# A two-layer RWKV-7 / attention hybrid on one core: the recurrence's L and R in one tile, 128-partition stream transposes, the product with v turned around, and a new order

## The chip, the cores and the metric

The kernel runs on one core of one Trainium2 chip. The metric is device time in microseconds of that core, the median of several executions. The core has TensorE (PE in the profile, with its weight loads as PEld), VectorE (DVE), ScalarE (ACT), GpSimd (POOL), and SyncE (SP), whose queue issues the weight transfers. Each engine runs its own instructions in program order, and waits on semaphores of the others.

## The reference, cut to what matters

Two layers of: a SwiGLU block, a mixer with three branches, a second SwiGLU block, on 256 tokens of width 1024. The branches are an RWKV-7 recurrence run forwards and backwards (8 heads of 64), global attention and window attention (8 query heads and 2 key/value heads each).

```
for l in range(2):
    x = x + 0.5 * swiglu(rmsnorm(x, ffn1_norm[l]), ffn1_w_up[l], ffn1_w_down[l])
    p = rmsnorm(x, mix_norm[l]) @ w_in[l]
    p_rwkv, p_ga, p_wa, p_gate = split(p)
    # recurrence, per head, in both directions of time:
    #   sa    = state @ a_t
    #   state = state * w_t + sa (x) b_t + v_t (x) k_t ;  y_t = state @ r_t
    y_a = rwkv_mixer(p_rwkv, ...)
    y_b = softmax(q k^T) v            # global, q and k normed and rotated
    y_c = window softmax with a sink  # 128 tokens to either side
    g = sigmoid(p_gate)
    x = x + (g0 * (y_a @ w_o_rwkv) + g1 * (y_b @ w_o_ga) + g2 * (y_c @ w_o_wa)) @ w_out
    x = x + 0.5 * swiglu(rmsnorm(x, ffn2_norm[l]), ffn2_w_up[l], ffn2_w_down[l])
return rmsnorm(x, final_norm)
```

## The kernel before, in words

**Weights.** Every weight is read once, in units of 128 x 1024 (`Net.unit`, lines 68 to 93). SyncE loads a unit into `w_raw`; ACT or DVE rounds it to `w_hi` (lines 61 and 63), and DVE or POOL forms the rest `w_lo` (line 92). Each big product is three matmuls (`mm3`): high by high, high by low, low by high. There are three `w_raw`, four `w_hi` and four `w_lo` buffers, so an engine that makes a `w_hi` can wait until PE has used up an older one.

**Mixer.** `Mixer.run` (line 976) is eight families of generators, and the string `ORDER` says which takes its next step: Q, projections of the two attentions; R, projections of the recurrence (tile `rk`, token shift in `shifted`, line 604); A, scores and softmax; V, the product with v (`pv`, line 509); K and P, preparation; 0 to 3, the four units of the recurrence (two pairs of heads, each forwards and backwards); O, its end; F, gates (`gt`) and output projections (`wo`), which are work for PE that can stand anywhere. The table `ENG` names the engine of each copy and, for each weight unit, who makes its two parts: v (ACT, DVE), p (ACT, POOL), w (DVE, POOL), x (DVE, DVE). Within the limits of the string, the framework's scheduler places the instructions of each engine.

**Product with v** (lines 509 to 543). Each pair of heads has its probabilities transposed on PE (`ptp`) and copied to the tile `PT`. Then, for each head, each half of the queries and each half of the keys, `PT` is the stationary operand, 128 x 128, and v is streamed with 64 columns: eight products per pair. The result `yv` has queries on the partitions; DVE multiplies it by the reciprocal of the softmax sum (line 538), PE transposes it back (`yTp`), and ACT and DVE split it into high and low parts.

**One unit of the recurrence** (`wkv`, line 719). PE forms the chunk products `Lp`; DVE masks the two halves of each bank into two tiles, `LA` and `LR` (lines 743 and 744, 128 x 256 each). After the backward unit of a pair, one triangular system is solved for both directions ("solve" from here on): four stream transposes of 32 partitions each bring the diagonal blocks of `LA` together in the tile `sol` (line 767), 28 small dependent DVE instructions (lines 775 and 776) solve it, further transposes bring it back (lines 780 and 785), and PE goes on with the products `gp` (line 791), `tp`, `gp`, `tp`, `lv`, `tx`, `rm`, `st` and `y`. `gp` and all behind it need the solve. There is one solve for each pair, so two in a mixer and four in the kernel. `LA` is one buffer for both directions of a pair; `LR` has two.

Of the kernel before, what the change touches and what calls it, by code (L numbers as in the profile page):

```python
# [288 lines left out]
class Mixer:  # L289
# [79 lines left out]
    def att_begin(self):  # L369
# [15 lines left out]
        at3 = self.t([128, 2048], "at3", tag="LA")  # L385
# [4 lines left out]
        self.t1 = at3[:, 1024:1664]  # L390
# [61 lines left out]
    def att_tools(self, kind):  # L452
# [10 lines left out]
        def turn():  # L463
# [45 lines left out]
        def pv(pr):  # L509
# [9 lines left out]
            if pr % 2 == 0:  # L519
                state["y"] = n.acc([128, 2, 4, 64], "yv")  # L520
            y = state["y"]
            for e in range(2):
                for t in range(2):
                    for kt in range(2):
                        first = pr % 2 + e + t + kt == 0
                        i = n.mm(y[:, t, 2 * (pr % 2) + e, :], self.PT[e][:, kt, 128 * t:128 * t + 128], qk[kt][:, v], start=first, stop=(kt == 1), skip_group_check=True)
                        if first:
                            state["first"] = i
                        else:
                            n.tc.add_manual_dep(i.ins, state["first"].ins.name, mybir.DependencyInfo(mybir.DependencyClass.NoSync, mybir.DependencyReason.DATA), reason="start of the bank")  # L530
# [7 lines left out]
            V.tensor_tensor(yt.rearrange("p t (h c) -> p t h c", c=64), y, den[:, :, hs].unsqueeze(3).to_broadcast([128, 2, 4, 64]), ALU.mult)  # L538
            p = n.bank([128, 2, 256], "yTp")
# [3 lines left out]
            n.split(p, yT[0][:, 2 * kv:2 * kv + 2, :], yT[1][:, 2 * kv:2 * kv + 2, :])  # L543
# [25 lines left out]
    def rwkv_begin(self):  # L569
# [4 lines left out]
        pad = [scr[:, 260 * i:260 * i + 258] for i in range(2)]  # L574
        for p in pad:
            nc.gpsimd.memset(p[:, 0:1], 0.0)
            nc.gpsimd.memset(p[:, 257:258], 0.0)
        self.pads, self.npad = pad, 0

    def rwkv_proj(self):  # L580
        nc, n, w = self.nc, self.n, self.a["w_in"][self.l]
        for g in (3, 1, 0, 2):
            for j0 in (0, 2):
# [16 lines left out]
                for j in range(nch):  # L600
                    self.shifted(g, j0 + j, acc[j])
                yield

    def shifted(self, g, j, acc):
        nc, n = self.nc, self.n
        ch = 4 * g + j
        dst = self.LG[:, j, :] if g == 3 else self.RKV[:, g, j, :]
        i = self.npad = self.npad + 1
        p = self.pads[i % 2]
        nc.scalar.activation(p[:, 1:257], acc, AF.Copy, scale=self.c2[:, ch:ch + 1])  # L610
        nc.vector.scalar_tensor_tensor(dst, acc, self.c1[:, ch:ch + 1], p[:, 0:256], ALU.mult, ALU.add)  # L611
        nc.vector.tensor_tensor(dst, dst, p[:, 2:258], ALU.add)
# [106 lines left out]
    def wkv(self, u):  # L719
# [28 lines left out]
        for i in range(2):  # L748
# [7 lines left out]
            for h in range(2):  # L756
                n.copy("av"[h], dst[E[h], 1], b[1][E[1 - h]])
# [301 lines left out]
```

## Time and profile before

| | us |
|---|---|
| median of 3 runs (1503.72 to 1505.63) | 1504.91 |
| time of the profiled execution | 1505.69 |
| span of the profiled execution, first to last instruction | 1503.8 |

The profiled execution's own time is 1.9 us more than its span, and 0.8 us above the median. Its mean granted TensorE clock was 0.98.

| stretch of the span, us | what runs |
|---|---|
| 0 to 202 | layer 0, first SwiGLU |
| 202 to 545 | layer 0, mixer: to 300 projections, to 360 attention and gates, then the recurrence with the gates |
| 545 to 569 | layer 0, product with w_out |
| 569 to 965 | layer 0, second SwiGLU, and layer 1, first SwiGLU |
| 965 to 1308 | layer 1, mixer and w_out |
| 1308 to 1504 | layer 1, second SwiGLU |

How to read the views. The groups of instructions give line, engine, operation, tile written <- tiles read, shapes, count | busy us, mean ns of one | idle time of the engine before them, and what ended it. The waits give who waited for whom: total us, times, longest. The windows give, for a stretch, busy time and count of each engine, the granted TensorE clock, the DMA share and GB/s. The timeline gives start us, length us, and in brackets the engine's idle time before the row. A product of two float32 operands is one row in the order of instructions and two records in the profile (the order has 128 rows of `yv`, the profile 256). Records of PE overlap, so the rate of a run of them is read from its start to the start of the next row, not from the length of one record.

### The profile page before, as it was taken

Reading aid. Unit: us, or ns where it says so; the run is one execution under the profiler, and the core shown is the slowest. Engines: PE = TensorE matmul, PEld = TensorE weight load, DVE = VectorE, ACT = ScalarE, POOL = GpSimd, SP = SyncE. Lnnn points to the kernel's source line nnn. Section 1 sums busy time; section 2 is a strip of 40 time slices with the busy share of each in tenths; the row PEclk is TensorE's granted clock in tenths of the full one; section 3 lists DMA queues with packets and bytes.
Section 4 is the critical chain, followed back from the end, with each engine's and each line's share of the span. In section 5 each row is a group of like instructions: output and inputs, shape, how many; then the busy total and the mean of one; then the engine's idle time right before and its main releaser. Section 6 shows DMA issues by size and latency. Waiting matters only on the chain.

```text
span 1503.8 us, 25092 instructions
## 1 busy us (share of the span) xinstructions
PE 1425.9 (95%) x10170; PEld 1167.8 (78%) x10170; DVE 925.7 (62%) x1384; ACT 701.9 (47%) x1109; POOL 224.5 (15%) x203
## 2 busy tenths in 40 slices
PE   8999999999797999999999999999997979999997
PEld 6888878877575778888888888788785758788886
DVE  5455468765859666555465554778657685755543
ACT  6444335764333246444354443466642332554443
POOL 0000033223214110000000000432242132100001
PEclk9999999999899899999999999999998989999999
DMA  7666656323313146666666666553242121576653
GB/s 220 195 198 189 189 149 187 109 85 106 106 51 98 53 133 182 185 181 190 186 182 184 182 185 193 152 170 105 78 125 87 44 86 58 153 213 182 194 182 112
DMA packets 113432, 220.19 MB, mean 146 GB/s; under 512 B 7362, under 2 KB 32164, under 8 KB 113316
## 3 DMA queue, kind: packets, MB, share of 16 engines
q1 hardware_dynamic: 111328, 215.08, 47.7%
q10 hardware_dynamic: 1508, 2.58, 0.6%
q8 instruction: 80, 1.31, 0.4%
q0 software_dynamic: 480, 0.93, 0.3%
q14 instruction: 36, 0.29, 0.1%
HBM read 217.51 MB, written 1.05 MB: 145 GB/s over the span
## 4 chain that ended last, share of the span: by engine, by line
PE 69%; DVE 14%; issue 5%; ACT 5%; DMA 4%; POOL 3%; SPq 0%; POOLq 0%; ACTq 0%; DVEq 0%
PE up L51 26%; PE dn L51 18%; PE gt L51 5%; DMA w_raw<-in_ffn_w_up 3%; DVE w_lo L92 3%; PE rk L51 3%; PE tp L54 2%; PE wo L51 2%; PE yv L51 2%; ACT w_hi L61 1%; DVE sol L775 1%; PE tx L51 1%; DVE sol L767 1%; DVE sol L776 1%; PE pj L51 1%
## 5 line engine op out<-in xcount | busy, mean ns | idle before, releaser
L92 DVE TENSOR_TENSOR w_lo<-w_raw,w_hi 128x1024 fp32r<-128x1024 f32 (+1 forms) x348 | 427.0, 1229 | 343.3 <-ACT w_hi L61 342.4
L61 ACT ACTIVATE w_hi<-w_raw 128x1024 fp32r<-128x1024 f32 (+1 forms) x376 | 394.6, 1051 | 469.1 <-PE up L51 175.0
L51 PE MATMUL up<-w_hi,hT 128*128 128x512 f32 x1408 | 443.5, 394 | 0.0
L51 PEld LDWEIGHTS up<-w_hi,hT 128*128 128x128 f32 x1408 | 265.3, 189 | 53.9
L51 PE MATMUL up<-w_lo,hT 128*128 128x512 f32 x704 | 274.5, 391 | 0.0
L51 PE MATMUL dn<-w_hi,aT 128*128 128x512 f32 x704 | 218.2, 390 | 0.0
L92 POOL TENSOR_TENSOR w_lo<-w_raw,w_hi 128x1024 fp32r<-128x1024 f32 (+1 forms) x62 | 147.5, 2383 | 228.1 <-ACT w_hi L61 146.1
L51 PEld LDWEIGHTS up<-w_lo,hT 128*128 128x128 f32 x704 | 132.7, 188 | 28.2 <-DVE w_lo L92 1.1
L51 PEld LDWEIGHTS dn<-w_hi,aT 128*128 128x128 f32 x704 | 131.7, 188 | 26.8
L51 PE MATMUL dn<-w_lo,aT 128*128 128x512 f32 x352 | 138.0, 392 | 0.0
L51 PE MATMUL gt<-w_hi,hT 128*128 128x512 f32 x384 | 135.8, 418 | 2.3 <-DVE w_hi L63 2.3
L51 PE MATMUL rk<-hT,w_hi 128*128 128x256 f32 x480 | 88.2, 285 | 2.5 <-DVE RKV L611 2.5
L51 PEld LDWEIGHTS gt<-w_hi,hT 128*128 128x128 f32 x384 | 73.8, 195 | 20.6 <-issue 3.0
L51 PE MATMUL gt<-w_lo,hT 128*128 128x512 f32 x192 | 80.5, 419 | 2.5 <-DVE w_lo L92 2.5
L142 POOL TENSOR_SCALAR stat<-stat 128x1 f32<-128x1 f32 x14 | 3.5, 254 | 511.1 <-ACT gh L138 495.0
L51 PEld LDWEIGHTS rk<-hT,w_hi 128*128 128x128 f32 x480 | 75.3, 191 | 4.4 <-DVE RKV L611 2.9
L51 PEld LDWEIGHTS dn<-w_lo,aT 128*128 128x128 f32 x352 | 66.1, 188 | 14.8 <-DVE w_lo L92 1.4
L51 PE MATMUL rk<-hT,w_lo 128*128 128x256 f32 x240 | 67.9, 284 | 1.4 <-POOL w_lo L92 1.4
L51 PE MATMUL wo<-w_hi,yT 128*128 128x512 f32 x192 | 65.5, 407 | 0.0
L51 PE MATMUL pj<-w_hi,hT 128*128 128x512 f32 x192 | 62.0, 397 | 2.1 <-DVE LG L611 2.1
L51 PEld LDWEIGHTS rk<-hT,w_lo 128*128 128x128 f32 x240 | 45.8, 191 | 1.8 <-POOL w_lo L92 1.8
L51 PEld LDWEIGHTS gt<-w_lo,hT 128*128 128x128 f32 x192 | 37.5, 195 | 11.6 <-DVE w_lo L92 3.2
(238 smaller groups left out, 1833.8 us busy)
## 6 DMA issues: line engine op xcount, KB each, us to landing
w_raw<-in_ffn_w_up SPq DMA_DIRECT2D x160, 512.0 KB
w_raw<-in_w_in SPq DMA_DIRECT2D x102, 512.0 KB
w_raw<-in_ffn_w_down SPq DMA_DIRECT2D x88, 512.0 KB
w_raw<-in_ffn_w_up SPq DMA_DIRECT2D x32, 256.0 KB
w_raw<-in_w_out SPq DMA_DIRECT2D x16, 512.0 KB
w_raw<-in_w_o_ga SPq DMA_DIRECT2D x8, 512.0 KB
w_raw<-in_w_o_wa SPq DMA_DIRECT2D x8, 512.0 KB
w_raw<-in_w_o_rwkv SPq DMA_DIRECT2D x8, 512.0 KB
```

The source lines that it names most:

```text
L51: return self.nc.tensor.matmul(*a, **k)
L54: return self.nc.tensor.transpose(*a, **k)
L61: self.nc.scalar.activation(out, in_, AF.Copy, scale=1.0 if scale is None else scale)
L92: self.engine(on[1]).tensor_tensor(o, r, h.bitcast(F32), ALU.subtract)
L142: nc.gpsimd.tensor_scalar(self.ss[:, c:c + 1], self.ss[:, c:c + 1], 1.0 / D, EPS, ALU.mult, ALU.add)
L767: V.transpose(sol[p0:p0 + 32], src[p0:p0 + 32, :, 32 * b:32 * b + 32].rearrange("p g (u t) -> p t u g", u=2))
L775: V.tensor_tensor(tv, Dm[:, s + 1:16, s:s + 1].to_broadcast([128, m, s]), Dm[:, s:s + 1, 0:s].to_broadcast([128, m, s]), ALU.mult)
L776: V.tensor_tensor(Dm[:, s + 1:16, 0:s], Dm[:, s + 1:16, 0:s], tv, ALU.add)
```

## The change

**One tile for L and R.** `LL` (128 x 2 x 8 x 192) holds `LR` in columns 0 to 127 and `LA` in 128 to 191, with two buffers. One DVE instruction of 128 x 512 masks a whole bank. The scratch tiles of the attention move into the same two buffers.

**128-partition transposes.** Before a solve, `blocks` copies the diagonal blocks of `LA` of both directions (32 partitions x 256, eight copies per solve, on ACT or DVE by the table entry K) into the second half of `scr`; then one stream transpose of 128 x 512 stands in for the four of 32 partitions.

**Product with v.** v is now the stationary operand (128 x 64) and `PT` is streamed with 256 columns, four products per pair; the two heads go to the two halves of the output partitions, in turn. The result `yp` has queries along the free dimension. The reciprocals are therefore spread, transposed on PE (`rdp`, as many transposes as `yTp` had) and copied (table entry J, two copies of 128 x 512 per key/value head), and one DVE product follows.

**Smaller edits.** The last addition of the token shift is done for two channel blocks at once. Copies that had a fixed engine take it from the table (entries K, C, U, Y, H, J).

**Order and table.** `ORDER` and `ENG` are new throughout.

```diff
-ORDER = 'QQQQQRRQQQRRQAQQRRRAAKAQRRPARRAKRKPVAVAARFRARFPVVAAAA...'
+ORDER = 'QQQQQQRRQQRQKRRRQQARARAQARAKARRRKPVVAAARFARARVVPPAAAAA...'
-        LR = self.t([128, 2, 8, 128], "LRt", tag="LR", bufs=2)
+        LL = self.t([128, 2, 8, 192], "LL", bufs=2)
+        LR, LA = LL[:, :, :, 0:128], LL[:, :, :, 128:192]
+        self.LAs[d] = LA
+        if d == 1:
+            scr = self.scr = self.t([128, 1024], "sol", tag="bk", bufs=2)
+            blk = scr[:, 512:1024].rearrange("p (n g t) -> p n g t", n=2, g=8)
+        def blocks(i):
+            for e in range(2):
+                for h in range(2):
+                    p = slice(64 * e + 32 * h, 64 * e + 32 * h + 32)
+                    n.copy(self.take("K"), blk[p, i], self.LAs[i][p, e, :, 32 * h:32 * h + 32])
+        if d == 1:
+            blocks(0)
...
-                V.tensor_tensor(LA[:, e, gs, :], b[e][:, :, 64:128], ...)
-                V.tensor_tensor(LR[:, e, gs, 0:64], b[e][:, :, 0:64], ...)
+                V.tensor_tensor(two(LL[:, e, gs, :])[:, :, 0:3:2, :], two(b[e]), ...)
+            if d == 1 and q == 1:
+                blocks(1)
...
-            for e in range(2):
-                src = LAp[:, e].rearrange("p n g t -> p (n g) t")
-                for b in range(2):
-                    p0 = 64 * e + 32 * b
-                    V.transpose(sol[p0:p0 + 32], src[p0:p0 + 32, :, 32 * b:32 * b + 32].rearrange("p g (u t) -> p t u g", u=2))
+            V.transpose(sol, blk.rearrange("p n g (u t) -> p t u (n g)", u=2))
...
-                state["y"] = n.acc([128, 2, 4, 64], "yv")
+                state["y"], state["first"] = n.acc([128, 2, 256], "yp"), [None, None]
...
-            for e in range(2):
-                for t in range(2):
-                    for kt in range(2):
-                        i = n.mm(y[:, t, 2 * (pr % 2) + e, :], self.PT[e][:, kt, 128 * t:128 * t + 128], qk[kt][:, v], ...)
+            for kt in range(2):
+                for e in range(2):
+                    i = n.mm(y[E[e], pr % 2, :], qk[kt][:, v], self.PT[e][:, kt, :], ...)
...
-            V.tensor_tensor(yt..., y, den[:, :, hs]..., ALU.mult)
-            p = n.bank([128, 2, 256], "yTp")
+            n.copy(self.take("J"), yt..., den[:, :, hs]...)
+            p = n.bank([128, 2, 256], "rdp")
...
-            n.split(p, yT[0][:, 2 * kv:2 * kv + 2, :], yT[1][:, 2 * kv:2 * kv + 2, :])
+            n.copy(self.take("J"), yt, p)
+            V.tensor_tensor(yt, y, yt, ALU.mult)
+            n.split(yt, yT[0][:, 2 * kv:2 * kv + 2, :], yT[1][:, 2 * kv:2 * kv + 2, :])
...
-        nc.vector.tensor_tensor(dst, dst, p[:, 2:258], ALU.add)
+        nc.vector.tensor_tensor(dst, dst, self.pads[:, :m, 2:258], ALU.add)
```

What the engines then run is read from the order of their instructions, in three places of layer 0.

VectorE, the first solve. `LAt` and `LRt` are the two tiles of before, `sol` is the scratch in which the system is solved, `T` are PE's transposes of the unit's operands. Before:

```order
L743 TENSOR_TENSOR LAt<-Lp_3229,consts 128x256
L744 TENSOR_TENSOR LRt<-Lp_3229,consts 128x4x64
L767 STREAM_TRANSPOSE sol<-LAt 32x512 x2
L63 COPY LRt<-T_3252 64x8x64
L767 STREAM_TRANSPOSE sol<-LAt 32x512 x2
L63 CAST w_hi<-w_raw 128x1024
L770 SCALAR_TENSOR_TENSOR sol<-sol,consts 128x256
L715 TENSOR_TENSOR BK<-kkh,tha 128x8x64
```

VectorE at the same place now:

```order
L752 TENSOR_TENSOR LL<-Lp_3169,consts 128x4x2x64
L752 TENSOR_TENSOR LL<-Lp_3170,consts 128x4x2x64
L63 COPY sol<-LL 32x256 x2
L772 STREAM_TRANSPOSE sol<-sol 128x512
L63 COPY LL<-T_3195 64x8x64
L775 SCALAR_TENSOR_TENSOR sol<-sol,consts 128x256
L63 CAST w_hi<-w_raw 128x1024
L780 TENSOR_TENSOR sol<-sol 128x14
```

Two block copies and one transpose stand where four transposes stood; the other six block copies of this solve are on ScalarE.

ScalarE, the second solve, before (`gth` are the gates' tanh):

```order
L61 ACTIVATE w_hi<-w_raw 128x1024
L61 ACTIVATE LRt<-T_4245 128x8x64
L61 ACTIVATE LRt<-T_4246 64x8x64
L61 ACTIVATE w_hi<-w_raw 128x1024 x3
L951 ACTIVATE gth<-gt_4224 128x512
```

ScalarE at the same place now:

```order
L61 ACTIVATE w_hi<-w_raw 128x1024
L61 ACTIVATE sol<-LL 32x256 x2
L61 ACTIVATE LL<-T_4224 128x8x64
L61 ACTIVATE sol<-LL 32x256 x2
L61 ACTIVATE LL<-T_4225 64x8x64
```

The four block copies of the backward direction stand behind a `w_hi` and around a copy of `T`.

TensorE, the end of the second solve, before:

```order
L51 MATMUL gt_4700<-w_hi,hT_65 128x512
L51 MATMUL gt_4700<-w_lo,hT_65 128x512
L51 MATMUL gt_4700<-w_hi,hT_66 128x512
L51 MATMUL gp<-Tn,LAt 32x32 x64
L51 MATMUL tp_4464<-sol,Tn 32x32 x32
L51 MATMUL tp_4503<-sol,Tn 32x32 x32
```

TensorE at the same place now:

```order
L51 MATMUL gt_4349<-w_hi,hT_66 128x512
L51 MATMUL gp<-Tn,LL 32x32 x64
L51 MATMUL gt_4350<-w_hi,hT_65 128x512
L51 MATMUL gt_4350<-w_lo,hT_65 128x512
L51 MATMUL gt_4350<-w_hi,hT_66 128x512
L51 MATMUL tp_4441<-sol,Tn 32x32 x32
L51 MATMUL tp_4480<-sol,Tn 32x32 x32
```

Three products of a gate have moved between `gp` and `tp`. By count of rows, from the last `Lp` to the first `gp` PE now has 66 big products in the first solve of a mixer (67 before) and 45 in the second (57 before), and 16 more transposes `T` in the first. From the decay preparation of the last unit (`lw`, `la`) to the second solve's `gp`, it has 101 (96 before).

Over the whole kernel DVE makes 52 `w_hi` (34 before) and POOL 50 `w_lo` (62 before).

More of the change, by code (lines that the diff above doesn't have):

```diff
@@ L469, in turn @@
                 nc.scalar.activation(kT[kind][E[e], e, :], p[E[e], 0, :], AF.Copy)
-                V.tensor_copy(kT[kind][E[1 - e], e, :], p[E[e], 0, :])
+                n.copy(self.take("H"), kT[kind][E[1 - e], e, :], p[E[e], 0, :])
             for i in range(2):
@@ L519, in pv @@
             if pr % 2 == 0:
-                state["y"] = n.acc([128, 2, 4, 64], "yv")
+                state["y"], state["first"] = n.acc([128, 2, 256], "yp"), [None, None]
             y = state["y"]
-            for e in range(2):
-                for t in range(2):
-                    for kt in range(2):
[L525 to L530, printed above, removed]
+            for kt in range(2):
+                for e in range(2):
+                    first = state["first"][e] is None
+                    i = n.mm(y[E[e], pr % 2, :], qk[kt][:, v], self.PT[e][:, kt, :], start=first, stop=(kt == 1), skip_group_check=True)
+                    if first:
+                        state["first"][e] = i
+                    else:
+                        n.tc.add_manual_dep(i.ins, state["first"][e].ins.name, mybir.DependencyInfo(mybir.DependencyClass.NoSync, mybir.DependencyReason.DATA), reason="start of the bank")
             if pr % 2 == 0:
@@ L537, in pv @@
             yt = self.yt[kv]
-            V.tensor_tensor(yt.rearrange("p t (h c) -> p t h c", c=64), y, den[:, :, hs].unsqueeze(3).to_broadcast([128, 2, 4, 64]), ALU.mult)
-            p = n.bank([128, 2, 256], "yTp")
+            n.copy(self.take("J"), yt.rearrange("p t (h c) -> p t h c", c=64), den[:, :, hs].unsqueeze(3).to_broadcast([128, 2, 4, 64]))
+            p = n.bank([128, 2, 256], "rdp")
             for r in range(2):
@@ L573, in rwkv_begin @@
         scr = self.t([128, 520], "projpad", tag="gth", bufs=2)
[L574 to L578, printed above, removed]
+        self.pads = scr.rearrange("p (i c) -> p i c", i=2)
+        nc.gpsimd.memset(self.pads[:, :, 0:258:257], 0.0)
     def rwkv_proj(self):
@@ L810, in wkv @@
         for e in range(2):
-            nc.scalar.activation(Gt[64 * e + 32:64 * e + 64], gp[64 * e + 32:64 * e + 64], AF.Copy)
+            n.copy(self.take("U"), Gt[64 * e + 32:64 * e + 64], gp[64 * e + 32:64 * e + 64])
         yield
@@ L817, in wkv @@
         for e in range(2):
-            V.tensor_copy(TT[64 * e:64 * e + 32, :, 32:64], tp[64 * e:64 * e + 32])
+            n.copy(self.take("U"), TT[64 * e:64 * e + 32, :, 32:64], tp[64 * e:64 * e + 32])
         b = n.bank([128, 8, 64], "lv")
@@ L824, in wkv @@
         for e in range(2):
-            (V.tensor_copy if e else nc.scalar.copy)(Z[E[e], e, :, 64:128], b[E[e]])
+            n.copy(self.take("Y"), Z[E[e], e, :, 64:128], b[E[e]])
         yield
@@ L833, in wkv @@
                 dst = Z[E[e], e, 4 * q:4 * q + 4, :].rearrange("p c (h t) -> p c h t", h=2)[:, :, ::-1, :]
-                (V.tensor_copy if e else nc.scalar.copy)(dst, b[E[e]].rearrange("p c (h t) -> p c h t", h=2))
+                n.copy(self.take("Y"), dst, b[E[e]].rearrange("p c (h t) -> p c h t", h=2))
             yield
```

45 lines of the change are left out of this document (19 added, 26 removed).

## The prediction

> **What bounds the kernel now.** I read the page's busy times, then the windows by stage, then who PE waits for inside the mixer, then the timelines there.
>
> ```profile
> span 1503.8 us, 25092 instructions
> PE 1425.9 (95%) x10170; PEld 1167.8 (78%) x10170; DVE 925.7 (62%) x1384; ACT 701.9 (47%) x1109; POOL 224.5 (15%) x203
> ```
>
> The windows by stage (us of the stage; busy us and count of PE, PEld, DVE, ACT, POOL; clock; DMA):
>
> ```profile
> 201.60:300.00 98.40, 91.75 (x594) 79.34 (x593) 77.88 (x124) 56.00 (x107) 33.80 (x40) 1.00 0.53 155
> 300.00:360.00 60.00, 58.45 (x369) 47.34 (x371) 35.79 (x75) 38.55 (x96) 21.22 (x12) 1.00 0.29 84
> 360.00:460.00 100.00, 88.53 (x1261) 69.93 (x1256) 68.24 (x134) 33.05 (x56) 20.52 (x11) 0.93 0.30 88
> 460.00:545.00 85.00, 73.69 (x1060) 60.35 (x1061) 63.22 (x120) 28.21 (x45) 26.22 (x13) 0.92 0.26 79
> 569.00:960.00 391.00, 387.98 (x1753) 315.68 (x1752) 215.73 (x244) 185.93 (x239) 14.49 (x31) 1.00 0.62 184
> ```
>
> The SwiGLU blocks (last row, 99% PE) are bound by PE, and the change doesn't touch them. In the mixer PE is 97% busy from 300 to 360, so work taken from PE there shows; from 360 to 545 it loses 22.8 us of 185. Of that, the largest wait is this one; its group for the whole kernel is below it:
>
> ```profile
> PE gp L51 <- DVE Tn L785: 12.5, 2, 7.3
> L51 PE MATMUL gp<-Tn,LAt 32*32 32x32 f32 x768 | 14.1, 224 | 29.3 <-DVE Tn L785 27.2 <-issue 2.1
> ```
>
> The four solves cost 27.2 us of PE's time: it has run out of gate products and waits for VectorE's chain. After each wait the clock is low, which makes the price a little higher:
>
> ```profile
> 400.00:410.00 10.00, 4.30 (x195) 3.93 (x196) 7.77 (x14) 0.15 (x1) 0.00 (x0) 0.52 0.34 108
> 490.00:500.00 10.00, 8.75 (x276) 7.54 (x278) 6.30 (x13) 3.31 (x8) 0.56 (x1) 0.53 0.17 56
> ```
>
> **The product with v.** PE's timeline, each row paired with the start of the next, gives rates:
>
> ```profile
> 349.17 2.00 PE L51 MATMUL yv<-att,at 128*128 128x64 f32 x16 [0.18 <-ACT at L61]
> 350.97 0.48 PE L51 MATMUL gt<-w_hi,hT 128*128 128x512 f32 x1
> ...
> 289.11 1.27 PE L51 MATMUL sc<-qkT 64*128 64x256 f32 x8
> 290.31 0.44 PE L54 MATMUL ptp<-head,at 128*128 128x128 f32 x2
> ...
> 426.16 0.92 PE L51 MATMUL st<-Zt,LRt 128*64 128x64 f32 x24
> 426.91 1.10 PE L51 MATMUL y<-LRt,Zt 128*64 128x64 f32 x32
> ...
> 496.41 1.91 PE L51 MATMUL bonp<-pz,consts 128*128 128x256 f32 x4
> 498.11 1.62 PE L51 MATMUL gatep<-LG,lora 128*128 128x256 f32 x4
> ```
>
> A `yv` record takes 1.80 / 16 = 0.112 us, so the 256 of them 28.8 us. The new form has 128 records of 256 columns on a 128 x 64 operand, which the trace doesn't show. Lower bound: `st` has that operand, two output halves in turn, and 0.75 / 24 = 0.031 us for 64 columns; four times the columns make 0.125, in all 16 us. Upper bound: `bonp`, 256 columns on a full operand, 1.70 / 4 = 0.425 us at clock 0.53, so 0.225 at full clock and 28.8 us: no gain. I take `sc`, 256 columns on half operands in turn, 1.20 / 8 = 0.150 us: 19.2 us, a gain of 9.6.
>
> Against it stand changes of the operand's shape, which the old form didn't need:
>
> ```profile
> 376.75 0.39 PE L51 MATMUL gt<-w_lo,hT 128*128 128x512 f32 x1
> 376.97 0.39 PE L51 MATMUL gt<-w_hi,hT 128*128 128x512 f32 x1
> 377.29 1.10 PE L51 MATMUL Lp<-ARV,BK 64*64 64x128 f32 x32
> ```
>
> Two `gt` start 0.22 us apart, `gt` and the differently shaped `Lp` 0.32: 0.10 us per change. The new order has ten groups of `yp` in a layer, so 40 changes in and out in all, 4 us. The term is -9.6 + 4 = **-5.6 us**; bounds -12.8 without a price for the changes, +4 with the upper bound.
>
> The Trainium skill's page "TensorEngine Tiling (Array Packing)", section Tiling Modes, speaks against this edit: changing the tiling mode drains TensorE. It gives no figure; the rows show 0.10 us, not an emptied pipeline (the `gt` record is 0.39 us long). Were every change to cost the rest of such a record, 0.39 - 0.22 = 0.17 us, 40 would be 7 us and the term -2.8.
>
> The spreading of the reciprocals adds 16 copies of 128 x 512 and takes nothing off PE (as many transposes). They need only the softmax sums, and lie on engines that are 60 and 64% busy in the window from 300 to 360: nothing; without that cover 16 x 0.69 = 11 us.
>
> **The solves.** VectorE's groups (and ScalarE's of 32 x 256, the nearest row for a block copy):
>
> ```profile
> L767 DVE STREAM_TRANSPOSE sol<-LAt 32x512 f32<-32x512 f32 x16 | 17.4, 1086 | 0.2
> L780 DVE STREAM_TRANSPOSE sol<-sol 128x512 f32<-128x512 f32 x4 | 4.2, 1038 | 0.1
> L803 ACT ACTIVATE TT<-sol 32x256 f32<-32x256 f32 x32 | 13.3, 414 | 47.1 <-DVE sol L799 46.8
> L743 DVE TENSOR_TENSOR LAt<-Lp,consts 128x256 f32<-128x256 f32 x32 | 13.3, 415 | 8.7 <-PE Lp L51 8.6
> L538 DVE TENSOR_TENSOR att<-yv,at 128x512 f32<-128x512 f32 x8 | 5.5, 691 | 15.2 <-PE yv L51 15.2
> L92 DVE TENSOR_TENSOR w_lo<-w_raw,w_hi 128x1024 fp32r<-128x1024 f32 x344 | 422.4, 1229 | 343.3 <-ACT w_hi L61 342.4
> ```
>
> Four transposes at 1.086 become one at 1.038: -3.3 us of chain. Two masks of 0.415 become one of 0.691 (`L538`, as many columns out of the same memory, is its nearest row): -0.14 per bank.
>
> *First solve of a mixer.* ScalarE has six block copies in a row, 6 x 0.414 = 2.5 us. They stand behind a copy of `T`, which I put at 0.7 (as `L538`), and that waits for PE's 16 transposes (0.5 at `st`'s 0.031): 3.7 us from the last `Lp`. VectorE's last two masks and two copies (0.4 each, as `L803`) take 2.2, so the transpose waits about 1.5 us: chain -3.3 + 1.5 = -1.8. PE's cover grows by 16 `T` (0.5) less one product (0.22): -0.3. Products now stand between `gp` and `tp`, where PE had nothing to do (the 2.1 of issue in the group above is one such gap): three fill 0.7. In all **-2.8 us** per layer of the 7.3. Bounds: -7.3 (the wait is gone) and +1 (the copies come later than the transposes were long).
>
> *Second solve.* VectorE is 63.22 of 85 us busy from 460 on, 9.2 of 10 just ahead of `gp`:
>
> ```profile
> 480.00:490.00 10.00, 4.89 (x34) 3.73 (x32) 9.21 (x30) 1.36 (x2) 4.02 (x2) 0.95 0.35 105
> ```
>
> From the last unit's preparation to `gp` its list gets shorter: -4.3 + 1.0 (transposes), -0.6 (eight masks of 0.415 to four of 0.691), -0.7 (one `w_hi`, row below) + 1.2 (one `w_lo`), + 0.4 (a block copy), and -2.2 for four instructions of 256 to 512 columns that now stand ahead of it (0.55 each, between `L743` and `L538`): -5.2 us. ScalarE's four copies come ahead of the transpose, + 1.4 on the chain. Between the last `Lp` and `gp` PE has twelve products less to cover the wait (2.6 us), but five more in the whole piece, work that it is spared elsewhere: I count these as equal. That leaves -3.8, say **-4 us** per layer; bounds -11 (PE's whole loss from 460 to 545) and +2 (the cover is lost, and little is gained).
>
> What can stretch the chain is seen here:
>
> ```profile
> 477.44 0.20 DVE L775 TENSOR_TENSOR sol<-sol 128x36 f32<-128x36 f32 x1
> 477.67 2.36 DVE L776 TENSOR_TENSOR sol<-sol 128x36 f32<-128x36 f32 x1
> ...
> 477.59 2.38 POOL L92 TENSOR_TENSOR w_lo<-w_raw,w_hi 128x1024 fp32r<-128x1024 f32 x1 [3.31 <-ACT w_hi L61]
> ```
>
> A `w_lo` on POOL holds a VectorE instruction that takes 0.2 us otherwise for 2.36. The new table has 12 fewer of them, but still some in the solves: no change taken.
>
> Both solves, two layers: 2 x (-2.8 - 4) = **-13.6 us**. With shorter waits the slow-clock stretches shorten: about 0.5 us at each, **-2**.
>
> **The rest.** VectorE makes 18 more `w_hi`, 13.4 us over two mixers where it is 60 to 79% busy by the windows:
>
> ```profile
> L63 DVE CAST w_hi<-w_raw 128x1024 fp32r<-128x1024 f32 x34 | 25.1, 743 | 13.1 <-PE gt L51 7.1 <-DMA w_raw<-in_w_in 2.8 <-issue 2.7
> ```
>
> Against them goes one of two additions in the token shift (15 per layer become eight, longer ones). I take nothing; up to 4 us per layer if the stage from 202 to 300 (VectorE 79%) becomes bound by it. POOL now has a `w_lo` between the sums of the last norm, 2.4 us, in a gap of 4.91:
>
> ```profile
> 202.22 0.30 POOL L142 TENSOR_SCALAR stat<-stat 128x1 f32<-128x1 f32 x1 [4.91 <-ACT gh L138]
> ```
>
> Nothing; without that gap 2.4 us per layer. Two `LL` buffers in place of one `LA` and two `LR`: no row has VectorE waiting for `LA`, so nothing. The fixed copies that now have an entry in the table: an engine change each, nothing.
>
> **The sum.** -5.6 - 13.6 - 2 = -21.2 us on the profiled execution's 1505.7: 1484.5. That execution was 0.8 above the median, so **1483.7 us**.
>
> **Rivals.**
> 1. *Deeper.* The waits for the solves nearly vanish (of 27.2, 25 go) and `yp` runs at its lower bound (-12.8): 1505 - 38 = 1467. For it: 101 products of cover before the second solve. Against it: only 45 of them behind the last `Lp`. 0.17.
> 2. *`yp` doesn't overlap.* The upper bound (+4), solves and clock as forecast (-15.6): 1493. For it: `bonp`. Against it: `st`. 0.13.
> 3. *The waits only move.* The order gives PE its cover elsewhere, and `gp` waits as long as before, while in the attention ACT's softmax, not PE, ends last: 1504. For it: twelve products fewer before the second `gp`. 0.06.
> 4. *Slower: the block copies wait behind ScalarE's `w_hi`.* Place: the ScalarE rows at the second solve, and the six copies at the first. ScalarE's waits in the mixer:
>
> ```profile
> ACT w_hi L61 <- PE gt L51: 13.0, 5, 5.3
> ACT LRt L61 <- PE T L54: 10.0, 4, 7.8
> ```
>
> A `w_hi` that waits for PE to free its buffer holds the copies up to 5.3 us. Four solves then lose 5.3 + 1.4 - 3.3 = 3.4 us each, +13.6, with -5.6 for `yp`: 1513. It makes the kernel slower from a lateness of about 3.3 us per solve. Against it: ScalarE is 33% busy there (33.05 of 100, 28.21 of 85). 0.09.
>
> **How the numbers follow.** Forecast 0.55 (its own range 1475 to 1494), rivals 0.17, 0.13, 0.06, 0.09. A measurement of this kernel tells differences over 0.2% (3 us) from none. Faster: 0.55 + 0.17 + 0.13 = 0.85; same 0.06; slower 0.09. The range leaves out rival 4, most of rival 3 and what lies below rival 1: 1467 to 1503.
>
> **What would show it.** In the profile after: `yp` records at about 0.15 us from start to start (0.125 and 0.225 are rivals); PE's wait for the solves at some 13 to 15 us in place of 27.2; one 128 x 512 transpose of about 1.04 us per solve; ScalarE's block copies ending within 2 us of the last mask; windows from 300 to 360 with PE still over 95% busy. The forecast is wrong if `gp` waits 25 us or more, if `yp` takes 0.2 us, or if the first 100 us of a mixer get longer by over 3 us.

## The result, and the profile after

The changed kernel takes 1461.1 us (median of 4 runs, 1459.5 to 1462.2), the kernel before 1505.3 (4 runs, 1503.7 to 1505.8): a ratio of 0.9708, 95% interval 0.9694 to 0.9723. That is 44 us less, where 21 were forecast; it lies below the range of 1467 to 1503. One run of e14 (1976 us) and one of e15 (4598 us) were in a slow state, and the times given for these two kernels leave them out.

The page's first part, after:

```profile
span 1459.2 us, 24811 instructions
PE 1407.0 (96%) x10042; PEld 1143.2 (78%) x10042; DVE 918.7 (63%) x1374; ACT 703.9 (48%) x1125; POOL 202.4 (14%) x181
```

PE is busy 18.9 us less, and idle 52.2 us (1459.2 - 1407.0) in place of 77.9 (1503.8 - 1425.9): 25.7 less. The SwiGLU blocks are as before (the group of `up` by `w_hi` is 442.9 us busy, before 443.5). The gain lies in the mixers. The windows of layer 0's mixer, cut at the same events in both kernels (first `pj`, first `Lp`, first `mean` at the end of the recurrence's first pair, first `up` of the next block); before, then after:

```profile
201.80:359.80 158.00, 149.80 (x953) 126.33 (x951) 113.47 (x198) 94.27 (x202) 54.81 (x51) 1.00 0.44 128
359.80:460.00 100.20, 88.73 (x1262) 70.11 (x1261) 68.24 (x134) 33.13 (x56) 20.72 (x11) 0.93 0.30 89
460.00:569.10 109.10, 97.79 (x1172) 79.38 (x1173) 78.20 (x142) 39.89 (x68) 27.39 (x17) 0.94 0.30 90
```

```profile
201.30:357.40 156.10, 149.21 (x909) 119.90 (x907) 123.42 (x216) 88.74 (x195) 47.16 (x43) 1.00 0.45 135
357.40:433.00 75.60, 71.27 (x1186) 56.86 (x1185) 54.24 (x110) 27.67 (x51) 17.32 (x8) 0.98 0.31 92
433.00:545.00 112.00, 105.19 (x1231) 85.71 (x1230) 77.79 (x144) 51.75 (x90) 26.73 (x16) 0.97 0.32 98
```

Work has moved between the three, so their lengths can't be compared one by one; PE's idle part can: 8.2, 11.5 and 11.3 us before, 6.9, 4.3 and 6.8 after (layer 1: 8.0, 10.0, 11.1, then 5.0, 5.4, 5.1). Projections and attention gave 4 us of idle time over both layers, the recurrence 22.

PE's waits, before, and the rows of after that answer to them:

```profile
PE gp L51 <- DVE Tn L785: 27.2, 4, 7.4
PE hb L54 <- ACT kkrs L632: 3.0, 2, 1.5
PE gt L51 <- DVE w_lo L92: 2.5, 2, 1.6
PE gt L51 <- DVE w_hi L63: 2.3, 1, 2.3
PE mean L51 <- DVE yacc L888: 2.2, 2, 1.8
```

```profile
PE gp L51 <- DVE Tn L790: 10.5, 4, 4.1
PE rk L51 <- DVE RKV L608: 4.2, 3, 2.0
PE T L54 <- DVE LL L63: 2.7, 2, 1.3
```

The solves' wait lost 16.7 us. The four rows shown behind it, 10.0 us, are gone altogether. Smaller ones came in their place: `rk` grew from 2.5 to 4.2, and `T` (2.7) is new.

**The product.** PE's timeline after:

```profile
287.29 1.08 PE L51 MATMUL yp<-at,att 128*64 128x256 f32 x8
288.31 0.44 PE L54 MATMUL rdp<-head,att 128*128 128x128 f32 x2
...
289.73 1.08 PE L51 MATMUL yp<-at,att 128*64 128x256 f32 x8
290.75 1.99 PE L51 MATMUL sc<-qkT 64*128 64x256 f32 x12
```

Eight records take 1.02 us, up to and with the change to the next shape: 0.1275 each, at the lower bound of 0.125.

**The solves.** First and second of layer 0, PE's last `Lp` and first `gp`; before (the first `Lp` stands in the prediction), then after:

```profile
403.60 1.61 PE L51 MATMUL gp<-Tn,LAt 32*32 32x32 f32 x105 [7.27 <-DVE Tn L785]
461.06 2.16 PE L51 MATMUL Lp<-ARV,BK 64*64 64x128 f32 x64
490.08 1.14 PE L51 MATMUL gp<-Tn,LAt 32*32 32x32 f32 x69 [5.19 <-DVE Tn L785]
```

```profile
369.09 1.10 PE L51 MATMUL Lp<-ARV,BK 64*64 64x128 f32 x32
393.28 1.35 PE L51 MATMUL gp<-Tn,LL 32*32 32x32 f32 x128 [1.19 <-DVE Tn L790]
448.86 1.36 PE L51 MATMUL Lp<-ARV,BK 64*64 64x128 f32 x32
467.16 1.07 PE L51 MATMUL gp<-Tn,LL 32*32 32x32 f32 x63 [4.04 <-DVE Tn L790]
```

From the end of `Lp` to `gp` the first solve takes 393.28 - 370.19 = 23.1 us in place of 25.2, the second 16.9 in place of 26.9. VectorE's first transpose in the second, before and after:

```profile
469.90 1.04 DVE L767 STREAM_TRANSPOSE sol<-LAt 32x512 f32<-32x512 f32 x1
```

```profile
453.19 1.13 DVE L772 STREAM_TRANSPOSE sol<-sol 128x512 f32<-128x512 f32 x1 [1.81 <-ACT sol L61]
```

It starts 3.0 us behind `Lp` in place of 6.7; from there to `gp` are 14.0 us in place of 20.2. In layer 1 the two solves take 23.1 us in place of 25.2, and 17.0 in place of 24.1.

### The profile page after: what moved, and what is told of

The parts are those of the page before. It is cut to its first block, busy times and chain, and to the rows that moved or that the text cites. A ratio compares the mean times of both kernels' runs of the same rounds, so it can differ in the third digit from the quotient of the medians.

```text
span 1459.2 us, 24811 instructions
## 1 busy us (share of the span) xinstructions
PE 1407.0 (96%) x10042; PEld 1143.2 (78%) x10042; DVE 918.7 (63%) x1374; ACT 703.9 (48%) x1125; POOL 202.4 (14%) x181
## 4 chain that ended last, share of the span: by engine, by line
PE 78%; issue 7%; DVE 6%; ACT 4%; DMA 2%; POOL 2%; SPq 0%; POOLq 0%; ACTq 0%; DVEq 0%
PE up L51 31%; PE dn L51 19%; PE gt L51 6%; PE rk L51 4%; PE wo L51 3%; PE pj L51 3%; PE tp L54 3%; DVE w_lo L92 1%; PE yp L51 1%; PE Lp L51 1%; POOL w_lo L92 1%; ACT w_hi L61 1%; DMA w_raw<-in_ffn_w_up 1%; DMA w_raw<-in_w_in 1%; PE sc L51 1%
## 5 line engine op out<-in xcount | busy, mean ns | idle before, releaser
L92 DVE TENSOR_TENSOR w_lo<-w_raw,w_hi 128x1024 fp32r<-128x1024 f32 (+1 forms) x360 | 443.7, 1233 | 348.3 <-ACT w_hi L61 346.9
L61 ACT ACTIVATE w_hi<-w_raw 128x1024 fp32r<-128x1024 f32 x358 | 379.9, 1063 | 463.8 <-PE up L51 172.4
L51 PE MATMUL up<-w_hi,hT 128*128 128x512 f32 x1408 | 442.9, 393 | 0.0
L92 POOL TENSOR_TENSOR w_lo<-w_raw,w_hi 128x1024 fp32r<-128x1024 f32 x50 | 123.6, 2475 | 148.4 <-ACT w_hi L61 91.5
L51 PE MATMUL gt<-w_hi,hT 128*128 128x512 f32 x384 | 139.0, 424 | 0.0
```

The costliest lines, as they stand in the source:

```text
L51: return self.nc.tensor.matmul(*a, **k)
L61: self.nc.scalar.activation(out, in_, AF.Copy, scale=1.0 if scale is None else scale)
L92: self.engine(on[1]).tensor_tensor(o, r, h.bitcast(F32), ALU.subtract)
```

## The experiments

Below, "worth" is a difference of ratios times 1505 us. "The chain" is the time from the last `Lp` of a solve to its `gp`, "cover" the products of 512 columns that the order of the instructions has in between.

### The parts, one by one and in pairs

"Tables" is the order and the engine table. The merged token shift goes with the changed code where both or one part was undone (e1, e2, e3), and stays out where one was put into the kernel before (e5, e6); it was not tried alone.

| kernel | us | ratio, 95% interval |
|---|---|---|
| product alone (e5) | 1500.1 | 0.9971, 0.9960 to 0.9982 |
| L and R alone (e6) | 1511.5 | 1.0052, 1.0033 to 1.0072 |
| tables alone (e4) | 1495.4 | 0.9927, 0.9899 to 0.9956 |
| product, L and R (e3) | 1509.0 | 1.0021, 1.0007 to 1.0035 |
| product, tables (e2) | 1480.6 | 0.9827, 0.9801 to 0.9854 |
| L and R, tables (e1) | 1471.0 | 0.9769, 0.9741 to 0.9796 |
| all three | 1461.1 | 0.9708, 0.9694 to 0.9723 |
| all, with the old engine table (e7) | 1509.9 | 1.0037, 1.0023 to 1.0052 |
| all, with the old order (e8) | 1509.8 | 1.0037, 1.0023 to 1.0052 |

**e1.** `pv` as in the kernel before:

```
-            for kt in range(2):
-                for e in range(2):
-                    i = n.mm(y[E[e], pr % 2, :], qk[kt][:, v], self.PT[e][:, kt, :], ...)
+            for e in range(2):
+                for t in range(2):
+                    for kt in range(2):
+                        i = n.mm(y[:, t, 2 * (pr % 2) + e, :], self.PT[e][:, kt, 128 * t:128 * t + 128], qk[kt][:, v], ...)
```

> The changed kernel (1461.1 us) with the old product with v alone put back (256 records of 64 columns, the reciprocals multiplied in before the transposes); order, engine table and LL stay new. Theory 'parts' (each edit is worth what it takes off TensorE's records or off a wait, whichever order it stands in): the records of the product from start to start fall by some 8 us in all with the change, TensorE has no slack to hide that in, so 1469, between 1467 and 1471. Rival 'hidden': in the attention the softmax ends last, and the product's records are covered; 1461 to 1463. Rival 'together': the new table counts on the shorter product and loses more than its records without it; 1473 or more.

The product is worth 9 us in the new order, with an interval of some 4 us to either side: as "parts" had it, at its upper end.

**e2.** `LL` in two tiles, two masks per bank, four transposes:

```
-            V.transpose(sol, blk.rearrange("p n g (u t) -> p t u (n g)", u=2))
+            for e in range(2):
+                for b in range(2):
+                    V.transpose(sol[p0:p0 + 32], src[p0:p0 + 32, :, 32 * b:32 * b + 32].rearrange("p g (u t) -> p t u g", u=2))
```

> The changed kernel with L and R in two tiles again (two masks per bank, four 32-partition transposes, no block copies); product, order and engine table stay new. Theory 'parts': VectorE's chain from the last product of Lp to the gate product gets longer by the transposes (4 x 1.09 against 1.04, 3.3 us) at the four solves, and TensorE, which already waits there (1.2 us at the first solve of a layer, 4.1 at the second), takes most of it: 4 x 2.5 to 3.3, 1471 to 1475. Rival 'order': the waits are short because of the order, and it has cover to spare; 1461 to 1465. Rival 'together': 1478 or more, with waits for the gate product as long as in the kernel before (27 us in all).

Worth 18 us, and the wait for `gp` is back at 25.3 us: "together", not "parts". The chain of the second solve, 16.9 us in the changed kernel, is some 21 here. The transposes add 3.3 us, and `w_lo` on GpSimd hold VectorE's instructions there for 4.8 us in place of 2.2; the wait for ScalarE's block copies (1.8 us) is gone.

**e3.** `ORDER` and `ENG` of the kernel before in the changed code.

> The changed kernel with the order and the engine table of the kernel before; the copies that had fixed engines go back to those (ScalarE makes all block copies; copies of reciprocals in turns). Product and LL stay new. Theory 'parts': product 8 us and LL 10 to 14 us off 1505.3 stay, so 1483 to 1488; the order and the table are worth the other 22 to 27. Rival 'order': the tables carry nearly everything and the edits of the code little: 1492 to 1500. Rival 'together': the code edits carry the gain and the tables only a few us: 1463 to 1472.

No theory had this: both edits of the code together lose 3 us in the old order.

**e4.** `ORDER` and `ENG` of the changed kernel in the kernel before.

> The kernel before with the new order and the new engine table alone (the copies that the table now names keep their fixed engines); product, L and R as before. Theory 'parts': the tables are worth 22 to 27 us, so 1478 to 1483. Rival 'order': nearly all, 1465 to 1472. Rival 'together': the order is made for the new code; without it it gives little or loses, 1495 to 1510.

Worth 11 us, at the better end of "together": the wait for `gp` is still 29.8 us.

**e5 and e6.** Each part of the code put into the kernel before.

> The kernel before with the new product with v alone (copies of the reciprocals in turns on ScalarE and VectorE), order, table, L and R as before. Theory 'parts': 1495 to 1499, since its records are 8 us shorter. Theory 'pairs' (after e1 to e4: an edit of the code gains only where the order puts work beside it; with the old order both edits together gave +4 us): the records get shorter and the time doesn't, 1502 to 1510, and the waits of TensorE elsewhere grow by what the records lose.

> The kernel before with L and R in one tile, the block copies on ScalarE and the one 128-partition transpose alone; product, order and table as before. Theory 'parts': 1491 to 1496 (four solves, each about 2.5 to 3.3 us less wait). Theory 'pairs': 1501 to 1508, the wait for the gate product still 24 to 30 us in all. Theory 'pool' (a w_lo on GpSimd beside VectorE's chain of small instructions stretches one of them by some 2 us; the number of them in a solve, not the transposes, sets the wait): the chain in the solves keeps three of them, so also 1501 to 1508, and the chain's small instructions (L767 to L799 of the changed code) take 12 to 13 us per solve against 9 in the changed kernel.

e5 is worth 4, between the two theories. e6 costs 8 us: not "parts", and 3 us more than "pairs" and "pool" allowed. Its order shows why the shorter chain brings nothing: cover fell with the chain, from 67 to 45 products at the first solves, from 57 and 56 to 48 and 46 at the second. At 0.231 us each (the mean distance of two `up` records) that is 5.1 and some 2.2 us; the waits only went from 7.3 to 6.7 at the first solves, and rose from 5.2 and 7.4 to 9.2 and 9.4 at the second. There GpSimd stands beside the chain; GpSimd's timeline, then VectorE's:

```profile
468.98 7.26 POOL L92 TENSOR_TENSOR w_lo<-w_raw,w_hi 128x1024 fp32r<-128x1024 f32 x3 [3.36 <-ACT w_hi L61]
```

```profile
469.03 2.62 DVE L778 SCALAR_TENSOR_TENSOR sol<-sol,consts 128x256 f32<-128x256 f32 x1
471.69 2.26 DVE L783 TENSOR_TENSOR sol<-sol 128x14 f32<-128x14 f32 x1
473.98 2.30 DVE L784 TENSOR_TENSOR sol<-sol 128x14 f32<-128x14 f32 x1
```

Three `w_lo` in a row hold three instructions, two of which take 0.17 us without them. In the changed kernel one `w_lo` holds an instruction there. The kernel before has such holds too: what held instructions take beyond their usual length is some 20 us over its four chains, and some 24 in e6. So they are a part of e6's 8 us at most.

**e7 and e8.** One table of the kernel before each.

> The changed kernel's code and order with the engine table of the kernel before (copies on their old engines). Theory 'order carries': 1463 to 1472. Theory 'engines carry' (fewer w_lo on GpSimd, copies in turns): 1485 to 1500. Theory 'pool': with the old table more w_lo fall on GpSimd beside the solves' chains, about one more per solve, each 2.1 us: 1469 to 1480.

> The changed kernel's code and engine table with the order of the kernel before. Theory 'order carries': 1497 to 1506 (as e3, 1509, less a few us). Theory 'engines carry': 1465 to 1480. Theory 'pool': the table alone takes some of the stretches away: 1490 to 1500.

Each loses all 44 us and 6 more, past what any of the theories gave: the order without its engine table is worth nothing, nor the other way round. In e8 the second solves are nearly those of e6, and the waits for `gp` are 26.1 us in all. In e7 the solves are good (wait for `gp` 13.7 us); the loss is at the start of the mixer and at its end. Its window from the first `pj` to the first `Lp`, and its largest wait there:

```profile
202.50:373.00 170.50, 155.52 (x913) 123.89 (x911) 120.42 (x198) 98.16 (x208) 56.14 (x48) 0.96 0.42 124
```

```profile
PE rk L51 <- DVE RKV L608: 10.2, 2, 5.5
```

That stage takes 170.5 us in place of 156.1: with the old engines the token shift comes late, and PE waits 5.5 us for it in one layer and 4.7 in the other. From the first `mean` to the next block it is 117.8 and 120.2 us in the two layers, in place of 112.0 and 108.7.

### More cover, and nothing else

**e9, e10, e11.** Weight units of the gates stand earlier in the order; in e9 and e11 `gp` also follows the last of them:

```
-ORDER = '...F3FO3F3223O2232F2332323323223F323OOOFFFFF'
+ORDER = '...F3FO3FFF3223O22322332323323223323OOOFFFFF'    (e10)
+                n.tc.add_manual_dep(i.ins, n.last.ins.name, ... NoSync ..., reason="cover")    (e9, e11)
```

> L and R in one tile alone (as e6, 1511.5 us), with more products put ahead of the gate product: in the order five weight units of the gates and outputs stand ahead of the first solve's end and three ahead of the second's, and the gate product follows the last of them. TensorE then has 72 products of 512 columns between the last Lp and gp in place of 45 (first solve), 75 and 84 in place of 48 and 46 (second). Theory 'cover' (the scheduler put as much work ahead of gp as it thinks the chain is long; with the shorter chain it took as much cover away as the chain lost, so the waits of 6.7, 9.2, 6.7 and 9.4 us stayed): 27 to 38 products more at 0.231 us are 6.2 to 8.8 us per solve, the waits fall from 32 us to under 6, and 1511.5 - 26 = 1485, or 1478 to 1490. Rival 'later': what is put there is missing behind gp, where TensorE waits for the later steps of the recurrence: 1500 or more. Rival 'clock': with the waits gone the half-clock stretches go too, 1470 to 1478.

> The changed kernel, with two weight units of the gates put earlier in the order, so that 60 products in place of 45 stand between the last Lp and gp of the second solve; nothing else. Theory 'cover': 15 x 0.231 = 3.5 us of the 4.0 and 4.1 us waits go, twice: 1461.1 - 7 = 1454, or 1453 to 1457. Rival 'later': the same time is waited for behind gp, 1460 to 1463. Rival 'pool': the two units bring their parts, made on GpSimd, into the chain and stretch it by as much again: 1460 to 1466.

> The kernel before with nothing but cover: six and three weight units put ahead of the solves' ends, gp behind the last of them. TensorE then has 84 products in place of 67 ahead of gp at the first solves, 75 and 66 in place of 57 and 56 at the second. Theory 'cover': 17 x 0.231 = 3.9 us at each first solve, 4.2 and 2.3 at the second: 14 us off 27, 1491, or 1488 to 1494. Rival 'later': 1500 to 1508. Rival 'pool': the w_lo of these units fall into the chains and stretch them: 1505 or more.

e9: 1503.6 us, 0.9999 (0.9983 to 1.0015). e10: 1477.5 us, 0.9817 (0.9802 to 0.9831), 16 us worse than the changed kernel. e11: 1508.6 us, 1.0025 (1.0009 to 1.0041). "Cover" misses in all three. "Later" has e9 right; e10 is far above its range, and e11 just above it and also in that of "pool". e9 is still 8 us better than e6. The wait for `gp` shrinks as it was meant to (in e9 from 32.1 to 2.2 us, in e10 from 10.5 to 2.9, in e11 from 27.2 to 14.5), and comes back one step on: in e9 PE waits 27.4 us for `Tn` at `tp`. In e9, PE:

```profile
398.23 1.34 PE L51 MATMUL gp<-Tn,LL 32*32 32x32 f32 x128 [0.59 <-DVE Tn L793]
405.18 1.08 PE L51 MATMUL tp<-sol,Tn 32*32 32x32 f32 x64 [5.61 <-DVE Tn L801]
```

and VectorE, which has to subtract between `gp` and `tp` (line 801):

```profile
397.63 0.77 DVE L793 STREAM_TRANSPOSE Tn<-sol 128x256 f32<-128x256 f32 x2
398.33 2.32 DVE L92 TENSOR_TENSOR w_lo<-w_raw,w_hi 128x1024 fp32r<-128x1024 f32 x2
400.56 1.28 DVE L981 SCALAR_TENSOR_TENSOR gth<-gth,wo 128x512 f32<-128x512 f32 x2
401.76 1.29 DVE L982 TENSOR_TENSOR merged<-merged,gth 128x512 f32<-128x512 f32 x2
402.96 1.22 DVE L92 TENSOR_TENSOR w_lo<-w_raw,w_hi 128x1024 fp32r<-128x1024 f32 x1
404.10 0.69 DVE L63 CAST w_hi<-w_raw 128x1024 fp32r<-128x1024 f32 x1
404.70 0.42 DVE L801 TENSOR_TENSOR Tn<-gp,Tn 128x256 f32<-128x256 f32 x1
```

The reader should see 6.4 us of other work queued on VectorE (398.33 to 404.70) between two links of the chain. PE can go on only when VectorE reaches the subtraction, so cover for one wait helps only if VectorE's list behind it is laid out for the new time; an order sets both. In e10 the same: PE waits 11.8 us for `Tn` behind `gp`, and 7.4 for `yT` at `wo`.

### GpSimd beside the chain

**e12.** e6 with `F17` from w to x, `F18` and `F28` to `F31` from p to v in `ENG` (VectorE makes those `w_lo`).

> L and R in one tile alone (as e6, 1511.5 us), with the six w_lo that GpSimd makes in and around the solves of a layer made by VectorE. The order of the instructions then has 67 products ahead of gp at the first solves in place of 45, 77 and 66 at the second in place of 48 and 46. Theory 'pool' (each w_lo on GpSimd beside the chain holds one of its small instructions for 2.1 us, two at the first and three at the second solve, and no order counts on that): the chain's small instructions fall from 11 to 13 us to some 9 and the waits from 32 us to 10 or less: 1485 to 1495. Rival 'VectorE': six more w_lo of 1.23 us on VectorE stand in the chain or ahead of it, and the chain gets as much longer as the cover: waits of over 20 us, 1503 to 1512.

1493.8 us, 0.9925 (0.9908 to 0.9941): 19 us better than e6. The chain's own instructions (all of `sol`) take 9.0 us per solve in place of 12.9 and 15.4, and the wait for `gp` fell from 32.1 us to 12.9. The time and these two marks are as "pool" had them. But the whole chain got no shorter: it takes 21.4, 26.1, 21.3 and 22.2 us at the four solves, in e6 20.7, 22.6, 20.7 and 22.5, since `w_lo` and `w_hi` of VectorE (5.6 to 12.8 us in a chain) stand in it now. The waits fell because cover rose, from 184 products at the four solves to 277, or 93 x 0.231 = 21 us. So e12 shows that the holds are gone, not what they alone cost.

**e13, e14.** The changed kernel with `F30`, then `F30` and `F31`, from p to v. **e15.** The kernel before with `F17` from w to x, and `F16`, `F18`, `F28` to `F31` from p to v.

> The changed kernel, with the one w_lo that GpSimd makes inside the second solve of a layer made by VectorE. The order has 50 products of 512 columns ahead of gp there in place of 45. Theory 'pool': the chain's small instructions take 9.1 us in place of 11.2, VectorE's own w_lo (1.23 us) may stand in the chain; the waits fall from 4.0 to some 2 us, 1461.1 - 4 = 1457, or 1455 to 1459. Rival 'chain': the wait moves behind gp, as in e10 where 60 products stood there: 1461 to 1470.

> The changed kernel, with the two w_lo that GpSimd makes in and at the end of the second solve of a layer made by VectorE; 56 products ahead of gp in place of 45. Theory 'pool': waits for gp near zero, and the steps behind it are no longer stretched either: 1452 to 1457. Rival 'chain': as e10 (1477), 1468 to 1478.

> The kernel before, with the seven w_lo that GpSimd makes in and around the solves of a layer made by VectorE. The order then has 97 products ahead of gp at the first solves in place of 67, 77 and 84 at the second in place of 57 and 56. Theory 'pool': the small instructions and transposes of the solve take some 12.3 us in place of 13.6 to 16.4, the waits of 27 us fall under 12, and 1505 - 12 = 1493, or 1488 to 1497. Rival 'chain': the cover put ahead is missing behind gp, 1502 to 1512.

e13: 1469.7 us, 0.9773 (0.9758 to 0.9787). e14: 1469.8 us, 0.9774 (0.9758 to 0.9790). e15: 1523.8 us, 1.0129 (1.0113 to 1.0146). All three miss "pool"; e13 and e14 lie in the range of "chain", but not by its mechanism, as the wait at `gp` itself grew (second solves of e13: 5.8 and 6.0 us in place of 4.0 and 4.1). In e13 a `w_lo` of VectorE stands in the chain (1.2 us). The `w_lo` of GpSimd that held an instruction there is gone, but the next two, which in the changed kernel start just ahead of the chain's end, now hold two of its instructions (2.25 and 2.26 us long): 2.0 us more. Here, and in the changed kernel:

```profile
465.34 4.66 POOL L92 TENSOR_TENSOR w_lo<-w_raw,w_hi 128x1024 fp32r<-128x1024 f32 x2 [1.69 <-ACT w_hi L61]
```

```profile
465.27 4.82 POOL L92 TENSOR_TENSOR w_lo<-w_raw,w_hi 128x1024 fp32r<-128x1024 f32 x2 [1.69 <-ACT w_hi L61]
```

They start alike, but `gp` starts at 472.4 in place of 467.2: from the first transpose to `gp` it is 17.0 us in place of 14.0. In e14 two `w_lo` and one `w_hi` more of VectorE, 3.1 us, make it 17.7. In e15 six or seven `w_lo` and three `w_hi` of VectorE, 9.4 to 10.6 us, stand in each chain, where one to three stood before, and the chains are 6 to 8 us longer. In none of the three did the holds go: the instructions of `sol` take 13.2 us at the second solves of e13 (11.2 in the changed kernel), 11.2 in e14, and 14.3 to 16.4 in e15 (13.6 to 16.4 before), as other `w_lo` of GpSimd fall beside them. So these runs don't tell what the holds cost. They show that a new maker for one unit moves the others, and that VectorE's own share can land in the chain.

**e16.** The changed kernel, with

```
+            for _ in range(5):
+                nc.gpsimd.tensor_tensor(scr[:, 832:1024], scr[:, 832:1024], scr[:, 832:1024], ALU.subtract)
```

> The changed kernel, with five subtractions of 128 x 192 on GpSimd beside the chain of each solve (on a piece of the scratch tile that is written anew later, so no value changes); the order on TensorE, VectorE and ScalarE stays. Theory 'pool': GpSimd is busy some 2.4 us more beside the chain, which gets longer by as much as VectorE is held, 2.1 us, and the waits for gp grow by that: 4 x 2.1 = 8.4, 1469.5, or 1466 to 1473. Rival 'chain': subtractions of GpSimd hold nothing up, or the stretch is hidden: 1460 to 1463.

1463.6 us, 0.9729 (0.9713 to 0.9745), 3 us worse: between the two theories. Five short subtractions stretch the chain by 0.7 to 0.9 us, not 2.1, and four times 0.8 is 3.2 us: here, where the order stays, what is added to the chains fits what is added to the time, though 3 us are at the edge of what these intervals tell apart. The waits for `gp` rose by more (10.5 to 16.8 us): at the first solves the stretch at half clock that lengthens the cover in the changed kernel is missing. No kernel tried here beats the changed one.

The Trainium skill's page "SBUF — State Buffer", section Who interferes with whom, says that a VectorE instruction with two inputs in SBUF and a GpSimd instruction that reads SBUF exclude each other, the later one waiting for the whole of the other. The rows agree: 0.17 us became 2.26 and 2.30 beside a `w_lo` of 2.4 us, and the subtractions of e16, 0.5 to 0.8 us each, held VectorE for little.

## Why the prediction was right and wrong

**The product** (-5.6; bounds -12.8 and +4). Right, with its parts moved. The records run at the bound from `st`, not at `sc`'s 0.150. Over all records, from each start to the next start without idle time, `yv` took 28.3 us and `yp` 20.5: -7.8. Of the 20.5, 128 x 0.1275 = 16.3 is the rate of the rows above, with the change to the next shape in it; the other 4.2 stand in rows that are broken up or wait. The 20 records of other tiles that stand just ahead of a `yp` take some 2.3 us more than others of their kind, so that the term is about -5.5. The Trainium skill's page "TensorEngine Tiling (Array Packing)", section Tiling Modes, states that a change of tiling mode drains TensorE. In this trace these 20 changes cost some 0.1 us each, as the prediction had put them, and not the whole of a record of 0.39 us. Undone in the new order, the product is worth 9 us; put into the old one, 4.

**First solve** (-2.8 per layer). The chain was right: -2.1 us measured, -1.8 forecast, with ScalarE's copies of blocks 2.4 us behind the last mask, some 0.4 more than the 2 I gave them:

```profile
370.23 1.29 DVE L752 TENSOR_TENSOR LL<-Lp,consts 128x512 f32<-128x512 f32 x2 [2.69 <-PE Lp L51]
```

```profile
371.36 2.55 ACT L61 ACTIVATE sol<-LL 32x256 f32<-32x256 f32 x6
```

The wait fell by 6.1 us, since the cover grew by more than the 16 `T`: 1.3 us of it are a wait of `T`, and 3.4 us ran at half clock, which makes cover longer without any work. That part is luck: in e16, with the same order, the stretch is missing, and the same solve waits 3.6 us.

**Second solve** (-4 per layer). Too small. The chain got 9.9 us shorter in layer 0 (7.1 in layer 1), not 3.8. The transposes are 3.3 of it, as forecast. The larger part is GpSimd, of which the prediction says "no change taken". Ahead of the first transpose, where 3.7 us went, two instructions of VectorE are held in the kernel before; VectorE's rows, then GpSimd's:

```profile
463.92 2.83 DVE L973 TENSOR_TENSOR merged<-merged,gth 128x512 f32<-128x512 f32 x1
468.00 1.98 DVE L63 CAST w_hi<-w_raw 128x1024 fp32r<-128x1024 f32 x1
```

```profile
463.82 2.38 POOL L92 TENSOR_TENSOR w_lo<-w_raw,w_hi 128x1024 fp32r<-128x1024 f32 x1 [1.20 <-PE Lp L51]
467.08 2.35 POOL L92 TENSOR_TENSOR w_lo<-w_raw,w_hi 128x1024 fp32r<-128x1024 f32 x1 [0.87 <-ACT w_hi L61]
```

Without a `w_lo` beside them these two take 0.68 and 0.69 us: 3.4 us of hold. Behind the transpose two more are held (2.36 us from 477.67, 2.24 from 484.24), 4.2 us; in the changed kernel one is (from 455.06), 2.2 us. That makes 7.6 us of hold before and 2.2 after, some 5.5 of the 9.9. Over the four chains the holds come to some 20 us before and 8 after. Cover fell by 12 `gt`, where I had counted it as equal; so of the 9.9 us only 1.2 are that wait (3.3 in layer 1); 3.8 are other waits of PE in that piece (the `gt` rows above), which are gone, and the rest products that now stand elsewhere.

All four waits together went from 27.2 to 10.5 us, -16.7 where -13.6 was forecast. That the sums are so near is luck: the first solves gave 12.2 where 5.6 was forecast, the second 4.5 where 8 was.

**The clock** (-2). The mean clock, before and after:

```profile
core 0: 1503.8 us, clock 0.980
```

```profile
core 0: 1459.2 us, clock 0.991
```

At 0.5 in the slow stretches that is 60 us of them before and 26 after. Little of it was worth anything: 30 records of `gt` ran in them before, 31 after, and against the mean distance of their kind at full clock all large products in them lost 9.3 and 8.4 us. The term is about -1.

**The rest** (0). This is the step that failed: the order and the engine table were put at nothing beyond the two edits. With -16.7 for the solves, -7.8 for the product and -1 for the clock, 19 of the 44.6 us of span are left, and I had put nothing there. About 9 are other waits (25.7 of idle time less 16.7): `gt` for its weights, `hb`, `mean`, `pj`. Some 10 lie in the distances between other records, where a record of 0.39 us outlasts the start of the next by some 0.17 and a short wait doesn't show as idle: `gp` and `tp` together fell from 59.2 to 55.0 us, `pj` from 70.3 to 67.6, `sc` from 22.3 to 20.3, with as many records. What shortened each stays open. I had taken the order and the table as what carries the two edits, and neutral otherwise. The runs show that they carry the gain: both edits lose 3 us in the old order, and tables and edits apart are worth 11 - 3 = 8 us, together 44. Which entries do it is open; e7 and e8 say that neither table does it alone.

**The rivals.** "Deeper" (1467) came nearest, for other reasons: the waits for the solves fell by 16.7 of its 25 us, the product by 7.8 of its 12.8, and the rest made up for both. The fourth (slower) has its sign in one experiment, but not its mechanism: put into the old order, `LL` alone costs 8 us, with its chains 1.6 to 4.5 us shorter.

## What to carry to other kernels

Price an edit together with the order that it comes with: a shorter chain gains only where the work put beside it, on PE and on the engine that makes the chain, is laid out for the new length, and a scheduler can take away as much cover as the chain lost. Ask of each link of a chain what stands in its engine's list between it and the next, not only how long it is itself. Count work on GpSimd beside a chain of short VectorE instructions as part of the chain: where a 128 x 1024 subtraction met one here, it held it for 0.8 to 2.2 us.

## What the runs showed of the hardware

The same wait can cost very different amounts. In e2 the first solves of both layers have the same products and the same wait:

```profile
395.67 1.93 PE L51 MATMUL gp<-Tn,LAt 32*32 32x32 f32 x128 [5.30 <-DVE Tn L782]
```

```profile
1129.09 1.93 PE L51 MATMUL gp<-Tn,LAt 32*32 32x32 f32 x128 [5.33 <-DVE Tn L782]
```

and the windows around them, from the first `Lp` to the first `mean`:

```profile
358.00:441.20 83.20, 76.16 (x1181) 60.81 (x1180) 56.57 (x123) 25.83 (x46) 14.62 (x7) 0.88 0.26 77
1091.40:1167.80 76.40, 70.23 (x1182) 55.92 (x1181) 56.51 (x123) 25.89 (x46) 14.66 (x7) 0.98 0.28 84
```

After the first, the clock stayed at half for 20.5 us, after the second for 3.4, and the first window is 6.8 us longer. For the last 13.7 of the 20.5 us PE was not idle at all:

```profile
401.75:415.40 13.65, 13.65 (x204) 10.64 (x202) 5.43 (x9) 4.33 (x10) 0.00 (x0) 0.50 0.27 79
```

The Trainium skill's page "TensorE: Matmul & The Clock Gate", section Part 1: The HAM clock gate, has one busy window of some 3.4 us bring the full clock back. If PE's records are what counts as busy, this row speaks against it, four such windows long. Most of what PE ran there were products of 32 x 32 and 64 x 64 (`gp`, `tp`, `lv`); that these don't count as busy is a guess that was not tried.
